# PSUM banks, the written order and the gate's rows between the output projection and the MLP of a hybrid layer

## The chip, the cores and the metric

The kernel runs on one core of a Trainium2 chip. The metric is device time in microseconds of one execution of the whole program; several executions are timed and the median is given. Beside them one execution is recorded by the hardware profiler, and all rows below are from that one. The engines are TensorE (PE, with its weight loads as PEld), VectorE (DVE), ScalarE (ACT), GpSimd (POOL) and SyncE (SP), which here only issues loads and stores.

## What is computed

One layer of a bidirectional trunk, 128 context and 512 latent tokens of width 1024. A token mixer of three head groups (differential attention, a gated linear recurrence, grouped-query attention) ends in one output projection, and an MLP with squared ReLU follows. What the change touches is from the projection on:

```python
def _layer(x, mod, lp, li, rope, ctx):
    sh1, sc1, g1, sh2, sc2, g2 = jnp.split(mod, 6, axis=-1)
    m, own = _token_mixer(x * (1.0 + sc1) + sh1, lp, li, rope, ctx)   # ends in mixed @ w_out
    x = _layernorm(ALPHA * x + g1 * m, lp['ln1_g'], lp['ln1_b'])
    hid = jnp.square(jax.nn.relu((x * (1.0 + sc2) + sh2) @ lp['w_ff1']))
    x = _layernorm(ALPHA * x + g2 * (hid @ lp['w_ff2']), lp['ln2_g'], lp['ln2_b'])
    return x, own
```

`w_ff1` is 1024 x 4096, `w_ff2` 4096 x 1024, all in float32.

## The kernel before, in words

A float32 operand is split into a high part (a cast, `A.copy` on ScalarE, L91, L1284, L1336) and a low part (a subtraction on VectorE, L92, L1287, L1340), and a product is three matmuls (high x high, high x low, low x high). The 640 tokens are five row tiles `t` of 128; tile 0 is the context.

**Projection (`wo_gemm`).** For each row tile and each half of the 1024 columns 24 matmuls sum into one PSUM bank (`pswo`). `residual` (L1226, L1230) reads that bank on VectorE, multiplies by the gate's row and adds to `xn`; `half_stats`, `norm_stats` and `normalize` (ScalarE, L1255 to L1258) follow in the second half. `turn(t)` transposes the normalised row tile on TensorE into two banks `psh{t}0` and `psh{t}1`, four blocks of 128 columns each, and `h2(t, q)` moves them into the quarters `raws[i, j]` (`q00` to `q11`) while it scales and shifts: `q=0` on ScalarE (L1281), `q=1` on VectorE (L1279).

**First MLP matrix.** It runs in 16 units `u` of 256 columns by Strassen's scheme in Winograd's form, seven products `m1` to `m7` of 12 matmuls each in place of eight. The activations' four sums `s1` to `s4` and quarters `a11`, `a12`, `a22` are made once (`sums12`, `sum_hi`, `sum_lo`); the weights' four sums `t1` to `t4` are made per unit by `b_sums` on VectorE (L1311 to L1313), and split by `hi_(u, what, ..)` and `lo_(u, what, ..)`. `keep(u, i)` copies a bank's state to SBUF on ScalarE (L1459); `c11`, `c12`, `c21`, `c22` add such copies to a bank and apply the squared ReLU (VectorE L1472 and L1467, or ScalarE L1464 and L1465); `store` parks the result in HBM. `m6(u)` adds to the bank that `keep(u,1)` has read, so it waits for that copy. Units 0 and 1 run interleaved in an order of their own, from unit 2 on a loop runs.

**Second MLP matrix.** Rows of the hidden layer come back from HBM (`hidb`), each is split (`gh`, `gl`, buffers of eight rows), each pair of weight blocks is loaded (`wg_..r`, two buffers) and split (`wg_..h`, `wg_..l`), and five banks `psy` sum over 32 rows, for one half `n` of the columns and then the other. The first four rows are taken from the end of the first matrix (`pair_gemm`). `gate_rows("g2", n)` spreads the second gate over the partitions by two matmuls (L1213) and two ScalarE copies (L1214); only the residuals after the last row need it.

**What sets the order.** From `region` on, TensorE, ScalarE, VectorE and SyncE run their instructions exactly as the code is written; outside it a list scheduler places them. `region.close()` stands before `gate_rows("g2", 0)`, so the scheduler placed that call. Each engine works off its queue in order, and an instruction that waits for another engine's count holds all that stand behind it. A PSUM tile's bank is given by the pools: `outps` has eight banks in turn, then `ffps` takes two banks for each of the tags `x`, `z`, `y`, `f`, in the order in which the tags are first asked for, and a tile may be written when all readers of the tile that had the bank before are done. In the program as built the last tiles lie so: row tile 3's projection (`pswo13`) in bank 7, `psh20` in 6, `psh21` in 7, `pswo14` in 4, `psy0` in 5, `psh30` and `psh31` in 6 and 7.

## Time and profile before

| | us |
|---|---|
| median of 3 runs (lowest, highest) | 940.05 (936.37, 941.13) |
| the profiled execution's own time | 940.01 |
| its span in the trace | 938.2 |
| PE / PEld / DVE / ACT / POOL busy | 880.3 / 762.6 / 665.1 / 474.9 / 69.0 |
| mean granted TensorE clock | 0.975 |

The span is the time from the first to the last instruction of the trace; 1.8 us of the execution lie outside it. A busy share is a mean over stages with different limits. The granted clock is given as a share of 2.4 GHz; 0.5 is 1.2 GHz.

### The profile page before, as it was taken

The numbers are of one execution on the slowest core, as the hardware profiler recorded it, in microseconds if no ns is written. First come the engines' busy times: TensorE is split into PE (matmuls) and PEld (weight loads), VectorE is DVE, ScalarE is ACT, GpSimd is POOL, SyncE is SP. The second block draws the span as 40 slices with busy tenths as digits, with TensorE's granted clock in tenths as the row PEclk, the third lists the DMA queues.
The fourth block names the chain that finished last, engine by engine and source line by source line (L and its number), as shares of the span: only waits on it lengthen the run. The fifth ranks groups of instructions, "written<-read, shape, count | busy, mean of one in ns | idle before, by whom it ended". The sixth has DMA issues, their size and how long they took to land.

```text
span 938.2 us, 15408 instructions
## 1 busy us (share of the span) xinstructions
PE 880.3 (94%) x5941; PEld 762.6 (81%) x5941; DVE 665.1 (71%) x1232; ACT 474.9 (51%) x973; POOL 69.0 (7%) x136
## 2 busy tenths in 40 slices
PE   5989898999999998999988899999998999999996
PEld 3878786789889786677778899988997888888885
DVE  2369997988876878886579877676762874574448
ACT  3567665466664638761566544453553633243320
POOL 2200010210101010001000100110000000000000
PEclk7999998999999999999999999999999999999998
DMA  9951525432122211007102543456325863052202
GB/s 261 287 168 50 179 71 146 118 95 69 55 58 62 68 51 57 2 28 274 36 1 64 186 145 134 157 176 208 129 79 188 295 218 99 22 177 90 67 22 92
DMA packets 102314, 109.84 MB, mean 117 GB/s; under 512 B 6720, under 2 KB 82208, under 8 KB 102240
## 3 DMA queue, kind: packets, MB, share of 16 engines
q1 hardware_dynamic: 96256, 92.33, 32.0%
q0 software_dynamic: 5792, 16.44, 5.0%
q8 instruction: 47, 0.77, 0.3%
q14 instruction: 27, 0.22, 0.1%
q10 hardware_dynamic: 192, 0.08, 0.0%
HBM read 96.24 MB, written 12.58 MB: 116 GB/s over the span
## 4 chain that ended last, share of the span: by engine, by line
PE 67%; DVE 15%; DMA 8%; ACT 6%; issue 3%; SPq 1%; DVEq 0%; ACTq 0%
PE psx L1453 10%; PE psy L131 8%; PE psy L129 8%; PE psy L130 8%; PE psz L1453 5%; DMA wad<-in_w_ada 3%; PE psA L130 2%; PE psA L129 2%; PE psA L131 2%; PE psavA L731 2%; DVE b_st L561 2%; PE psy L1453 2%; DMA wf_r<-in_w_ff 2%; PE psavC L953 1%; DVE b_lqk L516 1%
## 5 line engine op out<-in xcount | busy, mean ns | idle before, releaser
L92 DVE TENSOR_TENSOR gl<-hidb,gh 128x640 fp32r<-128x640 f32 x54 | 43.7, 821 | 49.1 <-ACT gh L91 49.0
L91 ACT CAST gh<-hidb 128x640 fp32r<-128x640 f32 x54 | 38.6, 728 | 69.3 <-PE psy L130 61.9
L1453 PE MATMUL psx<-s,wf3h 128*128 128x320 f32 x256 | 58.9, 317 | 6.2 <-ACT kept L1459 3.0
L129 PE MATMUL psA<-wa_h,xh 128*128 128x384 f32 x160 | 54.9, 344 | 0.0
L131 PE MATMUL psA<-wa_h,xl 128*128 128x384 f32 x160 | 54.5, 342 | 0.0
L130 PE MATMUL psA<-wa_l,xh 128*128 128x384 f32 x160 | 54.2, 340 | 0.0
L1459 ACT COPY kept<-psx 128x320 f32<-128x320 f32 x48 | 20.5, 427 | 65.6 <-PE psx L1453 65.6
L1453 PEld LDWEIGHTS psx<-s,wf3h 128*128 128x128 f32 x256 | 44.1, 193 | 7.0 <-ACT kept L1459 3.3
L1340 DVE TENSOR_TENSOR wf3l<-wf_t,wf3h 128x2048 fp32r<-128x2048 f32 (+2 forms) x20 | 37.2, 1864 | 9.0 <-ACT wf3h L1336 9.0
L1453 PE MATMUL psx<-s,wf3l 128*128 128x320 f32 x128 | 40.3, 315 | 0.0
L1472 DVE TENSOR_TENSOR st<-psz,kept 128x320 f32<-128x320 f32 x32 | 15.7, 489 | 26.2 <-ACT kept L1459 13.7
L129 PE MATMUL pswo<-wo,mxh 128*128 128x512 f32 x80 | 32.1, 403 | 0.4 <-ACT wo L91 0.4
L130 PE MATMUL pswo<-wo,mxh 128*128 128x512 f32 x80 | 31.7, 397 | 0.8 <-DVE wo L92 0.8
L709 DVE TENSOR_REDUCE nmA<-pssA 128x1 f32<-128x768 f32 x32 | 30.2, 951 | 2.2 <-PE pssA L707 1.8
L129 PEld LDWEIGHTS psA<-wa_h,xh 128*128 128x128 f32 x160 | 30.1, 188 | 1.9 <-issue 1.2
L1336 ACT CAST wf3h<-wf_t 128x2048 fp32r<-128x2048 f32 (+2 forms) x20 | 30.9, 1554 | 1.3 <-DVE wf_t L1312 0.9
L131 PE MATMUL pswo<-wo,mxl 128*128 128x512 f32 x80 | 31.5, 393 | 0.0
L1518 POOL DMA_DIRECT2D hd<-st x28 | 15.3, 546 | 219.3 <-ACT st L1465 120.4
L711 ACT ACTIVATE pA<-pssA,nmA 128x768 f32<-128x768 f32 x32 | 28.8, 903 | 3.3 <-DVE nmA L709 2.8
L130 PEld LDWEIGHTS psA<-wa_l,xh 128*128 128x128 f32 x160 | 30.2, 189 | 0.2
L131 PEld LDWEIGHTS psA<-wa_h,xl 128*128 128x128 f32 x160 | 30.1, 188 | 0.2
L1453 PE MATMUL psz<-s,wf3h 128*128 128x320 f32 x128 | 29.2, 315 | 0.0
(671 smaller groups left out, 2760.8 us busy)
## 6 DMA issues: line engine op xcount, KB each, us to landing
wad<-in_w_ada SPq DMA_DIRECT2D x32, 512.0 KB, 4.8
wf_r<-in_w_ff SPq DMA_DIRECT2D x32, 512.0 KB, 4.7
hd<-st POOLq DMA_DIRECT2D x28, 320.0 KB, 3.6
hidb<-hd SPq DMA_DIRECT2D x28, 320.0 KB, 4.7
adaw<-in_w_ada SPq DMA_DIRECT2D x32, 256.0 KB, 5.3
wa_r<-in_w_in SPq DMA_DIRECT2D x48, 128.0 KB, 2.7
wo_raw<-in_w_out SPq DMA_DIRECT2D x8, 512.0 KB, 6.5
x<-in_x_sample SPq DMA_DIRECT2D x8, 256.0 KB, 4.9
```

The source lines that it names most:

```text
L91: A.copy(hi, src)
L92: V.tensor_tensor(lo, src, f32(hi), op=ALU.subtract)
L129: PE.matmul(ps, s[0], m[0], start=start, stop=False)
L130: PE.matmul(ps, s[0], m[1], start=False, stop=False)
L131: PE.matmul(ps, s[1], m[0], start=False, stop=stop)
L561: V.scalar_tensor_tensor(dst, st[r, c, :], dec[r, c : c + 1], u(r, c), op0=ALU.mult, op1=ALU.add)
L709: V.tensor_reduce(nm, ps[:, 0:NKEY], axis=AX.X, op=ALU.max, negate=True)
L711: A.activation(pr, ps[:, 0:NKEY], AF.Exp, bias=nm, accum_out=sm[:, col : col + 1])
L1336: A.copy(h, src)
L1340: V.tensor_tensor(l, src, f32(h), op=ALU.subtract)
L1453: PE.matmul(ps, a_[:, k, :], b_[:, k, :], start=start and k == 0 and i == 0, stop=k == 3 and i == 2, skip_group_check=True)
L1459: A.copy(t, U[u].ps["x"][:, 0:HALF])
```

## The change

Five edits between the projection's second half and the end of unit 1, and one in the second matrix:

1. The tags of `ffps` are asked for in the order `x z f y` in place of `x z y f`. As built, `psh20` then lies in bank 4 and `psh21` in 5, `pswo14` in 6, `psy0` in 7, `psh31` in 5, `psh30` in 4. The banks' former tiles are those of row tile 1 and of the turn of tile 0; `pswo13` in bank 7 has `psy0` behind it.
2. `h2(0, 1)` runs on ScalarE and no longer on VectorE. `hi_(0, 3)` (the cast of unit 0's weight sums, 128 x 2048) stands before `h2(0, 0)` on ScalarE and no longer after `normalize(1)`. `lo_(0, 3)` keeps its place on VectorE.
3. The last turns: `turn` takes a list of quarters; tile 3's two are placed around `m2(0)`, tile 4's come before `m1(1)`. `h2(2, 1, 1)` comes before `residual(4)`, `h2(4, 1)` before the sums `s1` and `s2`; `keep(0, 1)` comes after tile 4's `h2` on ScalarE, and the cast `hi_(1, 3, 0, 2)` after `s1`'s.
4. The end of units 0 and 1: `b_sums` is cut into its first two and its last instruction. `c11(1)` moves from before `c22(1)` to after `c12(0)`, `b_sum4(2)` to after `lo_(2, 3, 0, 2)`, `c12(1)` to before `lo_(2, 3, 3, 4)`.
5. `gate_rows("g2", 0)` is called within the region, in the loop's pass for row 18.

```diff
-    def turn(t, bank="f"):
-        for q in range(2):
+    def turn(t, bank="f", qs=(0, 1)):
+        for q in qs:
...
-                if q:
+                if q and t:
                     V.tensor_scalar(dst, src, a2[:, kk, v : v + 1], b2[:, kk, v : v + 1], op0=ALU.mult, op1=ALU.add)
                 else:
                     A.activation(dst, src, AF.Identity, scale=a2[:, kk, v : v + 1], bias=b2[:, kk, v : v + 1])
...
     def b_sums(u, pool, tag):
+        b_sums3(u, pool, tag)
+        b_sum4(u)
+
+    def b_sums3(u, pool, tag):
         g = U[u]
         r = g.r
         g.t = t = pool.tile([P, 4, 4, P], F32, tag=tag, name=f"wf_t{u}")
         V.tensor_tensor(t[:, 0:2], r[:, :, :, 1, :], r[:, 0].rearrange("p k c n -> p c k n"), op=ALU.subtract)
         V.tensor_tensor(t[:, 2], r[:, 1, :, 1, :], t[:, 0], op=ALU.subtract)
-        V.tensor_tensor(t[:, 3], r[:, 1, :, 0, :], t[:, 2], op=ALU.subtract)
+
+    def b_sum4(u):
+        g = U[u]
+        V.tensor_tensor(g.t[:, 3], g.r[:, 1, :, 0, :], g.t[:, 2], op=ALU.subtract)
...
-            for b in "xzyf":
+            for b in "xzfy":
                 fps[0].tile([P, 512], F32, tag=b, name=f"ps_{b}")
...
             hi_(0, 2)
-            lo_(0, 3)
...
             normalize(0, mvs[0])
+            f3[0] = [wop.tile([P, 4, 4, P], F32R, tag=tag, name=f"wf3{p}0") for p, tag in (("h", "wr"), ("l", "w3"))]
+            hi_(0, 3)
         elif t == 1:
             h2(0, 0)
             h2(0, 1)
             normalize(1, mvs[1])
-            f3[0] = [wop.tile([P, 4, 4, P], F32R, tag=tag, name=f"wf3{p}0") for p, tag in (("h", "wr"), ("l", "w3"))]
-            hi_(0, 3)
+            lo_(0, 3)
...
             hi_(1, 2, 0, 1)
+            h2(2, 1, 1)
...
-    def c21(u):
+    def c21(u, last=True):
         relu2(st[:, u % 2, 0, HALF:NTOK], U[u].ps["x"][:, 0:HALF], True)
-        store(u, 0)
+        if last:
+            store(u, 0)
...
     m1(0)
-    keep(0, 1)
+    turn(3, qs=(1,))
+    m2(0)
     h2(2, 0, 1)
+    turn(3, qs=(0,))
     lo_(1, 1)
-    h2(2, 1, 1)
-    m2(0)
-    turn(3)
-    normalize(4, mvs[4])
-    m1(1)
-    turn(4, "z")
     h2(3, 1)
     lo_(1, 2, 0, 1)
+    normalize(4, mvs[4])
+    turn(4, "z")
+    h2(3, 0)
+    h2(4, 0)
+    h2(4, 1)
+    m1(1)
     m2(1)
-    h2(3, 0)
+    keep(0, 1)
     keep(1, 1)
     sums12(0, 192)
-    h2(4, 0)
-    h2(4, 1)
-    hi_(1, 3, 2, 3)
     parts("s2")
     sum_hi("s2", s2r, 0, 192)
-    hi_(1, 3, 0, 2)
+    hi_(1, 3, 2, 3)
...
     lo_(1, 3, 2, 3)
+    hi_(1, 3, 0, 2)
...
+    sum_hi("s4", s2r)
     c11(0)
-    sum_hi("s4", s2r)
...
     m3(0)
-    c11(1)
+    c21(1, False)
     c22(1)
-    c21(1)
     lo_(2, 1)
     m3(1)
+    b_sums3(2, wop, "w2")
+    hi_(2, 3, 2, 3)
+    lo_(2, 3, 2, 3)
     lo_(2, 2, 0, 1)
     c12(0)
-    b_sums(2, wop, "w2")
-    hi_(2, 3, 2, 3)
-    lo_(2, 3, 2, 3)
     hi_(2, 3, 0, 2)
+    c11(1)
+    store(1, 0)
     lo_(2, 3, 0, 2)
+    b_sum4(2)
     hi_(2, 3, 3, 4)
+    c12(1)
     lo_(2, 3, 3, 4)
     hi_(2, 2, 1, 2)
-    c12(1)
     lo_(2, 2, 1, 2)
...
+            if n == 0 and m == 20:
+                g2r = gate_rows("g2", 0, [fps[0].tile([P, 512], F32, tag=b, name=f"psabg2{b}") for b in "xy"])
             if n == 0 and m >= 8:
                 alpha_rows(m - 8)
...
             region.close()
-        g2r = gate_rows("g2", n, [fps[0].tile([P, 512], F32, tag=b, name=f"psabg2{b}") for b in "xy"] if n == 0 else None)
+        else:
+            g2r = gate_rows("g2", n)
```

TensorE before, from m1(0) to the start of m6(0). psx0 and psy0 are m1(0) and m2(0), psx1 and psy1 m1(1) and m2(1); psh3 and psh4 are the turns of row tiles 3 and 4.

```order
L1453 MATMUL psx0_5605<-a11_5333,b11_0_5123 128x320 x12
L1453 MATMUL psy0_5606<-a12_5334,wf12h_5471 128x320 x12
L1268 MATMUL psh30_5643<-ident_65,xn_5096 128x128 x4
L1268 MATMUL psh31_5648<-ident_65,xn_5096 128x128 x4
L1453 MATMUL psx1_5607<-a11_5333,wf12l_5472 128x320 x12
L1268 MATMUL psh40_5669<-ident_65,xn_5096 128x128 x4
L1268 MATMUL psh41_5674<-ident_65,xn_5096 128x128 x4
L1453 MATMUL psy1_5608<-a12_5334,wf12l_5472 128x320 x12
L1453 MATMUL psx0_5605<-s2_5712,wf3h0_5433 128x320 x2
```

The same place in the changed kernel.

```order
L1461 MATMUL psx0_5609<-a11_5333,b11_0_5123 128x320 x12
L1268 MATMUL psh31_5625<-ident_65,xn_5096 128x128 x4
L1461 MATMUL psy0_5610<-a12_5334,wf12h_5472 128x320 x12
L1268 MATMUL psh30_5646<-ident_65,xn_5096 128x128 x4
L1268 MATMUL psh40_5661<-ident_65,xn_5096 128x128 x4
L1268 MATMUL psh41_5666<-ident_65,xn_5096 128x128 x4
L1461 MATMUL psx1_5611<-a11_5333,wf12l_5473 128x320 x12
L1461 MATMUL psy1_5612<-a12_5334,wf12l_5473 128x320 x12
L1461 MATMUL psx0_5609<-s2_5711,wf3h0_5379 128x320 x2
```

All four turns now stand before unit 1's products, and none of the matmuls is new.

VectorE before, from s4's low part to the low part of unit 2's last weight quarter. The st rows with psz0, psy1 and psz1 are the sums of c22(0), c11(1), c22(1), c12(0) and c12(1) in that order; wf_t2 is b_sums(2).

```order
L1287 TENSOR_TENSOR s41_5821<-s2r_5603,s40_5820 128x1280
L1472 TENSOR_TENSOR st_5822<-psz0_5742,kept_5601 128x320
L1472 TENSOR_TENSOR st_5822<-psy1_5608,kept_5601 128x320
L1472 TENSOR_TENSOR st_5822<-psz1_5774,kept_5601 128x320
...
L1340 TENSOR_TENSOR wf12h_5471<-wf_r2_5723,wf12h_5471 128x512 x2
L1472 TENSOR_TENSOR st_5822<-psz0_5742,kept_5601 128x320
L1311 TENSOR_TENSOR wf_t2_5900<-wf_r2_5723 128x1024
L1312 TENSOR_TENSOR wf_t2_5900<-wf_r2_5723,wf_t2_5900 128x512
L1313 TENSOR_TENSOR wf_t2_5900<-wf_r2_5723,wf_t2_5900 128x512
L1340 TENSOR_TENSOR wf3l0_5434<-wf_t2_5900,wf3h0_5433 128x512
L1340 TENSOR_TENSOR wf3l0_5434<-wf_t2_5900,wf3h0_5433 128x1024
L1472 TENSOR_TENSOR st_5822<-psz1_5774,kept_5601 128x320
```

The same place in the changed kernel, from c22(1) on.

```order
L1480 TENSOR_TENSOR st_5822<-psz1_5774,kept_5605 128x320
L1347 TENSOR_TENSOR wf12h_5472<-wf_r2_5722,wf12h_5472 128x512
L1315 TENSOR_TENSOR wf_t2_5890<-wf_r2_5722 128x1024
L1316 TENSOR_TENSOR wf_t2_5890<-wf_r2_5722,wf_t2_5890 128x512
L1347 TENSOR_TENSOR wf3l0_5380<-wf_t2_5890,wf3h0_5379 128x512
L1480 TENSOR_TENSOR st_5822<-psz0_5742,kept_5605 128x320
L1480 TENSOR_TENSOR st_5822<-psy1_5612,kept_5605 128x320
...
L1347 TENSOR_TENSOR wf3l0_5380<-wf_t2_5890,wf3h0_5379 128x1024
L1320 TENSOR_TENSOR wf_t2_5890<-wf_r2_5722,wf_t2_5890 128x512
L1480 TENSOR_TENSOR st_5822<-psz1_5774,kept_5605 128x320
```

c11(1) went behind c12(0), the last weight sum behind the low part of the first two, and c12(1) ahead of the low part of the last.

ScalarE before, at the change to the second matrix. st is the last squared ReLU, g20 are the gate's rows, wg0_2h and gh0.. high parts of weights and hidden rows.

```order
L1464 ACTIVATE st_5822<-st_5822 128x320
L1465 ACTIVATE st_5822<-st_5822 128x320
L1214 COPY g200_8297<-psabg2x_8295 128x512
L1214 COPY g201_8300<-psabg2y_8296 128x512
L91 CAST wg0_2h_7740<-wg0_2r_7738 128x1024
L91 CAST gh02_7745<-hidb2_7712 128x640
```

ScalarE in the changed kernel, at the rows 17 to 20 of the second matrix.

```order
L91 CAST gh017_8107<-hidb17_7727 128x640
L91 CAST wg0_18h_8130<-wg0_18r_8128 128x1024
L91 CAST gh018_8135<-hidb18_7728 128x640
L1214 COPY g200_8141<-psabg2x_8139 128x512
L1214 COPY g201_8144<-psabg2y_8140 128x512
L91 CAST gh019_8165<-hidb19_7729 128x640
L91 CAST wg0_20h_8188<-wg0_20r_8186 128x1024
```

The two copies moved behind sixteen rows' casts; on TensorE their matmuls stand after row 17's, where before they stood before row 2's.

## Rows read from the trace of the kernel before

**Rows 1.** The page, part 1: busy time of each engine, its share of the span, and its instructions.

```profile
PE 880.3 (94%) x5941; PEld 762.6 (81%) x5941; DVE 665.1 (71%) x1232; ACT 474.9 (51%) x973; POOL 69.0 (7%) x136
```

**Rows 2.** Who waited for whom, TensorE alone, over the whole run: what waited, for what, us in total, times, longest us. Of the rows left out between the first and the second, one is m6(0)'s (3.0 us, on s L1284); one of them and one ahead of the third belong to the first half of the program.

```profile
PE psx L1453 <- ACT kept L1459: 3.0, 1, 3.0
...
PE psh L1268 <- DVE 1.18920711500272131_5542 L1226: 2.6, 1, 2.6
...
PE psy L129 <- ACT gh L91: 2.5, 1, 2.5
```

**Rows 3.** TensorE in order of time, 474 to 546 us: start us, us, engine, line, operation, out<-in, count, and in brackets the idle time before it and what ended it. The psh rows are the turn of row tile 2; pswo at 479 to 485 is the projection of row tile 4; psx<-a,b is m1(0); psx<-s,wf3h at 498 and 499 are the first two matmuls of m6(0), at 524 the first of m6(2).

```profile
475.34 0.66 PE L1268 MATMUL psh<-ident,xn 128*128 128x128 f32 x4 [0.24 <-ACT xn L1258]
478.64 1.11 PE L1268 MATMUL psh<-ident,xn 128*128 128x128 f32 x4 [2.64 <-DVE 1.18920711500272131_5542 L1226]
479.40 0.77 PE L129 MATMUL pswo<-wo,mxh 128*128 128x512 f32 x1
...
482.01 0.40 PE L130 MATMUL pswo<-wo,mxh 128*128 128x512 f32 x1
...
485.65 0.39 PE L131 MATMUL pswo<-wo,mxl 128*128 128x512 f32 x1
485.88 1.92 PE L1453 MATMUL psx<-a,b 128*128 128x320 f32 x12
...
498.41 0.63 PE L1453 MATMUL psx<-s,wf3h 128*128 128x320 f32 x1 [2.97 <-ACT s L1284]
499.23 0.63 PE L1453 MATMUL psx<-s,wf3h 128*128 128x320 f32 x1 [0.19 <-DVE s L1287]
...
524.66 0.56 PE L1453 MATMUL psx<-s,wf3h 128*128 128x320 f32 x2 [3.02 <-ACT kept L1459]
```

**Rows 4.** Stretches of 2 us, 460 to 534 us: stretch and its length, then busy time (and instructions) of PE, PEld, DVE, ACT, POOL, then the granted TensorE clock, DMA share and GB/s.

```profile
478.00:480.00 2.00, 1.36 (x6) 1.27 (x7) 1.93 (x3) 0.00 (x0) 0.00 (x0) 0.50 0.00 0
480.00:482.00 2.00, 2.00 (x7) 1.59 (x6) 1.74 (x8) 1.59 (x4) 0.00 (x0) 0.66 0.00 0
...
524.00:526.00 2.00, 1.34 (x8) 1.34 (x9) 1.93 (x3) 2.00 (x4) 0.54 (x1) 0.94 0.41 95
526.00:528.00 2.00, 2.00 (x10) 2.00 (x9) 2.00 (x3) 1.57 (x2) 0.00 (x0) 0.50 1.01 315
```

**Rows 5.** All engines in order of time, 462 to 500 us, columns as in rows 3; of it ScalarE and VectorE around the first turned tile. L1281 and L1279 are h2 on ScalarE and on VectorE, L1336 and L1340 hi_ and lo_, L1258 the end of normalize, L1226 the first step of a residual.

```profile
462.85 1.51 ACT L1281 ACTIVATE q<-psh,b,a 128x128 f32<-128x128 f32 x4 [0.75 <-PE psh L1268]
...
465.46 1.25 ACT L1258 ACTIVATE xn<-xn,mva 128x1024 f32<-128x1024 f32 x1
466.61 1.89 ACT L1336 CAST wf3h<-wf_t 128x2048 fp32r<-128x2048 f32 x1
468.53 2.29 DVE L1340 TENSOR_TENSOR wf3l<-wf_t,wf3h 128x2048 fp32r<-128x2048 f32 x1 [2.53 <-ACT wf3h L1336]
470.74 0.68 DVE L1226 TENSOR_TENSOR 1.18920711500272121_5475<-pswo,g 128x512 f32<-128x512 f32 x1
```

**Rows 6.** VectorE in order of time, 474 to 546 us, columns as in rows 3: the residuals of row tiles 3 and 4, the low part (two pieces) that m6(0) waits for, and s4's low part.

```profile
477.90 0.68 DVE L1226 TENSOR_TENSOR 1.18920711500272131_5542<-pswo,g 128x512 f32<-128x512 f32 x1
...
486.08 0.69 DVE L1226 TENSOR_TENSOR 1.18920711500272141_5592<-pswo,g 128x512 f32<-128x512 f32 x1 [2.88 <-PE pswo L131]
...
497.62 1.55 DVE L1287 TENSOR_TENSOR s<-s2r,s 128x768 fp32r<-128x768 f32 x2
...
511.69 1.49 DVE L1287 TENSOR_TENSOR s<-s2r,s 128x1280 fp32r<-128x1280 f32 x1 [0.41 <-ACT s L1284]
```

**Rows 7.** ScalarE in order of time, 474 to 546 us, columns as in rows 3: normalize(4)'s end, the first square of c12(1), and the copy keep(2,1) that m6(2) waits for.

```profile
490.24 1.24 ACT L1258 ACTIVATE xn<-xn,mva 128x1024 f32<-128x1024 f32 x1
...
523.32 0.47 ACT L1464 ACTIVATE st<-st 128x320 f32<-128x320 f32 x1 [1.26 <-DVE st L1472]
...
524.20 0.41 ACT L1459 COPY kept<-psx 128x320 f32<-128x320 f32 x1
```

**Rows 8.** TensorE in order of time, 698 to 732 us, columns as in rows 3: the gate's first matmul, and the first and the thirteenth matmul of the next pair of hidden rows.

```profile
719.13 0.39 PE L1213 MATMUL psabg2x<-grows,sel 128*128 128x512 f32 x1
...
722.25 0.50 PE L129 MATMUL psy<-wg_2h,gh 128*128 128x512 f32 x1 [2.50 <-ACT gh L91]
...
727.13 0.40 PE L130 MATMUL psy<-wg_2l,gh 128*128 128x512 f32 x1
```

**Rows 9.** ScalarE in order of time, 698 to 745 us, columns as in rows 3: the first of the gate's copies and the first cast of that pair.

```profile
719.56 0.59 ACT L1214 COPY g<-psabg2x 128x512 f32<-128x512 f32 x1 [9.64 <-PE psabg2x L1213]
...
720.52 1.06 ACT L91 CAST wg_2h<-wg_2r 128x1024 fp32r<-128x1024 f32 x1
```

**Rows 10.** SyncE's queue in order of time, 698 to 745 us: the issue of the first loads of that pair (start us, us of the issue).

```profile
708.41 0.38 SPq L1760 DMA_DIRECT2D wg_2r<-in_w_ff  x1
708.84 0.94 SPq L1764 DMA_DIRECT2D hidb<-hd  x2
```

**Rows 11.** All work on the tiles hidb between 705 and 730 us, its last row: time of a load from issue to landing.

```profile
DMA to landing us min/median/max: 4.3/5.2/8.8
```

**Rows 12.** All work on the tile wg_2r, its last row: time of that load from issue to landing.

```profile
DMA to landing us min/median/max: 3.6/3.7/3.7
```

**Rows 13.** Groups of instructions between 730 and 800 us: line, engine, operation, out<-in, count | busy us, mean ns of one | idle time of the engine just before, and what ended it.

```profile
L92 DVE TENSOR_TENSOR gl<-hidb,gh 128x640 fp32r<-128x640 f32 x21 | 17.2, 822 | 14.9 <-ACT gh L91 14.8
L91 ACT CAST gh<-hidb 128x640 fp32r<-128x640 f32 x20 | 14.5, 727 | 29.2 <-PE psy L130 25.3 <-DVE wg_16l L92 2.7 <-DMA hidb<-hd 1.2
```

## The prediction

> **What bounds the kernel now.** I read the busy shares first, then the waits of TensorE, then its instructions in order of time at the three waits that the edits touch. TensorE is busy for 880.3 of 938.2 us [rows 1], so a gain must come from its idle time or from stretches at the lower clock. Two of the three waits shown lie before m6(2) and before the second pair of hidden rows, the third is that of a turn [rows 2]. In order of time the reader sees how each begins: `psh21` may only be written when `residual(3)` has read bank 7, which it begins at 477.90 [rows 6], so TensorE idles 2.64 us and then runs the projection's last row tile at first at a clock of 0.50 and 0.66 [rows 3, 4]; before m6(2) it idles 3.02 us for `keep(2,1)` [rows 3]; and before the second pair it idles 2.50 us [rows 8], because ScalarE stood 9.64 us in front of the gate's copies [rows 9].
>
> **The turn's wait.** After the change `psh21` lies in a bank whose tile has long been read, and `pswo14` starts when the turn ends. `psh20` started at 475.34 [rows 3]; two turns of 0.4 us and a slip of 0.3 (below) put that at 476.1 against 479.40. A matmul at the full clock takes 0.2275 us, (485.65 - 482.01) / 16 [rows 3]; 24 take 5.46 us, where the slow start made them 6.48, 479.40 to 485.88 [rows 3]. m1(0) then starts at 481.6 in place of 485.88: **-4.3 us**.
>
> **What moves ahead of it.** ScalarE is free at 462.10, since it idled 0.75 us before 462.85 [rows 5]. It now does the cast (1.89) first, then two `h2` of 1.51 each [rows 5] where VectorE did the second. `normalize(1)` fills the time from the end of `h2(0,0)`, 464.36, less waits 2.14 us, to 466.71 [rows 5]; behind cast and both `h2` it ends near 468.85. Turn 1 is late by the 0.3 us used above. In return VectorE no longer waits 2.53 us before `lo_(0,3)`, and `residual(2)` starts near 468.8, not 470.74 [rows 5]. So VectorE reaches `residual(3)` earlier too, at some 476.5 against 477.90 [rows 6], and nothing that TensorE needs before m1(0) comes later.
>
> **How much reaches m6(0).** `residual(4)` waits for the projection (2.88 us of idle) and starts at 486.08 [rows 6]. It now stands behind `h2(2,1,1)`, 1.1 us, and starts near 482.8. `normalize(4)` ended at 491.48 [rows 7], held up by an `h2` and a copy that stood ahead of it on ScalarE; it ends near 487.3, TensorE turns tile 4 there, `h2(4,1)` follows at 488.5 to 489.9, the four sums end at 493.1, and the low part that m6(0) waits for at 494.5 in place of 499.17 [rows 6]. The second matmul of m6(0) goes from 499.23 [rows 3] to 494.6, -4.6 us. TensorE waits some 0.7 us longer in total there than before, since the turn of tile 4 now is waited for. The VectorE chain keeps this: `s4`'s low part ended at 513.18 [rows 6]; I take 508.3, **-4.9** (-4.6 to -5.3).
>
> **The end of units 0 and 1 gives some back.** From there to `keep(2,1)` it took 11.0 us, 513.18 to 524.20 [rows 6, 7]. In the new order VectorE waits twice for a ScalarE cast, which itself stands behind the relu of c12(0) and the squares of c12(1) (0.47 us each [rows 7]); I get 0.75 and 1.1 us of such idle, less 0.5 us of work moved behind the copy: 12.4 us. `keep(2,1)` then starts at 520.7 and m6(2) at 521.1 instead of 524.66 [rows 3]: **-3.6 us** net. TensorE reaches this point early and waits 4.5 to 4.9 us in place of 3.02, so its idle time hardly shrinks; VectorE's and ScalarE's chain is the bound here, and what edit 1 saves on TensorE is worth only what it saves on that chain. If the new order costs nothing the term is -4.9; if the shorter TensorE time only turns into waiting, it is 0. I choose -3.6 as the value that follows from walking the queues. From unit 2 on TensorE is the bound, and the shift is kept.
>
> On the restart rows show a clock of 0.94 in the first 2 us after the 3.02 us wait and 0.50 in the next two [rows 4]. So the wait already costs the low clock, some 1.8 us, and a longer wait costs it once more, not twice; I price it at zero difference. The Trainium skill, page "TensorE: Matmul & The Clock Gate", section "What's actually happening", says that the throttled state is the default and that activity releases it; by that rule a longer wait restarts every one of m6(2)'s matmuls at the low clock, and the term would be -2.5 by my estimate in place of -3.6. The 0.94 shows that this trace did not do so after 3.02 us.
>
> **The gate's rows.** Before, ScalarE stands from 709.9 to 719.56 in front of the copies, because their matmuls wait in TensorE's queue to 719.13 [rows 8, 9]. The loads for the next pair were issued at 708.41 and 708.84 [rows 10] and land 3.7 us [rows 12] and 4.3 to 8.8 us later [rows 11], at the latest at 717.6. So without the copies the casts are done before TensorE comes, and it goes on at 719.12 at the full clock. The thirteenth matmul of the pair, where it is back at the full rate, comes at 719.12 + 12 x 0.2275 = 721.85 rather than 727.13 [rows 8]: -5.28, less 0.46 for the two gate matmuls, which still run later: **-4.8 us**. Bounds: -3.0 (the wait alone is gone, the slow clock stays) and -5.3.
>
> **What it costs at row 18.** The copies now stand in ScalarE's queue behind row 18's cast and wait for TensorE to end row 17 (T). All later casts wait with them, and the lead of up to eight rows shrinks to one. The first row's cast follows 1.07 us (719.56 to 720.52 and the rest of the second copy [rows 9]) after T, then 0.73 and 0.82 us for high and low part [rows 13]; with semaphores row 19 is complete at T + 3.0, needed at T + 15 x 0.2275 + 0.46 = T + 3.87. The hard place is the end of the half: its last eight rows are summed bank by bank, so the first bank wants the last weight pair (rows 30 and 31) at T + 18.7. ScalarE has five pairs to do by then, each 1.06 + 2 x 0.73 = 2.52 us [rows 9, 13], 14.4 us with the copies, so 4 us are spare. But the pairs' loads have two buffers, and two loads in series lie before rows 30 and 31; with 3.7 us a load [rows 12] I walk the queues to T + 18.8. I take **+0.4** (0 to 1). If each of these loads takes 8.8 us [rows 11], it is 2 x 5.1 = 10.2 more, a wait of some 9 us and 2 more for the clock. The Trainium skill, page "PSUM — Partial Sum Buffer", section "Engine vs sequencer instructions", speaks against this edit: ScalarE's queue is strict first in, first out, so no ready cast may pass the waiting copy. The 9.64 us in front of one copy agree [rows 9]; by the rule the price above is due anew, at a place with more lead.
>
> The rest (stores, the order of c11 and c12, banks of later tiles) I cost at nothing: VectorE and ScalarE have idle time there behind a busy TensorE, and were that cover gone it would be the 0.5 us per moved instruction.
>
> **Sum.** 938.2 - 3.6 - 4.8 + 0.4 = 930.2 us of span; 1.8 us lie outside it: **932.0 us**. The profiled execution (940.01) stands at the median (940.05), so nothing is shifted.
>
> **Rivals.**
> - *The first stretch gains nothing:* the chain on VectorE and ScalarE keeps its time (the waits for the casts grow by all that is won), 935.6. For it: TensorE waits for other engines at both m6(0) and m6(2) [rows 3]. Against: `residual(4)` itself waits 2.88 us for TensorE [rows 6].
> - *More gain:* the end of units 0 and 1 costs nothing and row 18 neither, 930.3; without the restart's 1.8 us 928.5. Against it: the added waits follow from the queues.
> - *The lead is worth more than I think:* row 18 gives back 2.5 to 6 us, 934.2 to 938. For it: weights have two buffers, and my margin is 0.1 us.
> - *Slower:* the loads behind T take 8.8 us as the slowest did [rows 11], the last pair is 9 us late, and TensorE restarts slowly: +11 in place of +0.4, 942.6; with the first stretch at nothing as well 946. It decides, against the two gains of 8.4, once wait and clock exceed 8.4 us. Against it: the loads of weights took 3.7 us.
>
> **Chances.** Forecast (930 to 934.2) 0.58; no gain in the first stretch 0.13; more gain 0.09; lead worth more 0.14; slower 0.06. Leaving out a part of the slower and of the extreme cases gives 928.5 to 937.5. The bound between a change and none is 0.5%, what a measurement of this kernel can tell: 935.35 and 944.75. Faster: 0.58, 0.09, half of the first rival and a third of the lead's, 0.78; slower by more than that only the sum of two mishaps, 0.04; 0.18 within.
>
> **What would show it.** Right: no wait at `psh`'s second turn and a clock of 1.0 in the projection's last row tile; m1(0) near 481.6; m6(0) near 494; m6(2) near 521 behind a wait of over 4 us; no wait of ScalarE at 709, the second pair starting at the full clock right behind the first; ScalarE idle before `g` at row 18, and TensorE's wait near the last weight pair below 1 us. Wrong: m6(2) at 524 again, or a wait of several us for `gh` or `wg` in the last eight rows of the first half.

## The result, and the profile after

The changed kernel takes 933.02 us (median of 8 executions, 932.00 to 935.48), the kernel before 940.99 us in the same comparison: a ratio of 0.9917 (95% interval 0.9894 to 0.9941). The prediction was 932.0, range 928.5 to 937.5. The execution that was profiled took 932.00 us, the shortest of the eight, with a span of 930.2 us; predicted was a span of 930.2.

The page's first part, which answers to [rows 1]:

```profile
PE 878.0 (94%) x5941; PEld 760.8 (82%) x5941; DVE 663.0 (71%) x1228; ACT 475.9 (51%) x977; POOL 69.0 (7%) x136
```

TensorE's busy share did not move; what went is waiting and low clock. TensorE's waits over the whole run, cut to those behind the projection (columns as in [rows 2]):

```profile
PE psx L1461 <- ACT kept L1467: 4.5, 1, 4.5
...
PE psx L1461 <- ACT s L1284: 1.8, 1, 1.8
...
PE psh L1268 <- ACT xn L1258: 1.0, 1, 1.0
```

The waits for the residual and for `gh` in [rows 2] are gone, and the wait for `keep(2,1)` grew from 3.0 to 4.5 us. TensorE in order of time shows where (columns as in [rows 3], which answer to these rows; the last three are in the place of [rows 8]):

```profile
474.88 1.03 PE L1268 MATMUL psh<-ident,xn 128*128 128x128 f32 x8
475.67 0.48 PE L129 MATMUL pswo<-wo,mxh 128*128 128x512 f32 x1
...
481.24 1.92 PE L1461 MATMUL psx<-a,b 128*128 128x320 f32 x12
...
486.81 1.09 PE L1268 MATMUL psh<-ident,xn 128*128 128x128 f32 x8 [1.02 <-ACT xn L1258]
...
494.03 0.41 PE L1461 MATMUL psx<-s,wf3h 128*128 128x320 f32 x1 [0.41 <-DVE s L1287]
...
521.25 0.56 PE L1461 MATMUL psx<-s,wf3h 128*128 128x320 f32 x2 [4.45 <-ACT kept L1467]
...
715.60 0.39 PE L131 MATMUL psy<-wg_p,g 128*128 128x512 f32 x1
715.82 0.39 PE L129 MATMUL psy<-wg_2h,gh 128*128 128x512 f32 x1
...
718.09 0.39 PE L130 MATMUL psy<-wg_2l,gh 128*128 128x512 f32 x1
```

Both halves of turn 2 run in one piece, m1(0) starts at 481.24 (485.88 in [rows 3]), m6(0)'s second matmul at 494.03 (499.23), m6(2) at 521.25 (524.66), and the second pair of hidden rows follows the first without a gap. On VectorE and ScalarE, rows that answer to [rows 6, 7] and to the gate's copy in [rows 9]:

```profile
482.22 0.68 DVE L1226 TENSOR_TENSOR 1.18920711500272141_5596<-pswo,g 128x512 f32<-128x512 f32 x1
...
506.84 1.49 DVE L1287 TENSOR_TENSOR s<-s2r,s 128x1280 fp32r<-128x1280 f32 x1 [0.40 <-ACT s L1284]
...
513.34 0.69 DVE L1347 TENSOR_TENSOR wf3l<-wf_t,wf3h 128x512 fp32r<-128x512 f32 x1 [0.69 <-ACT wf3h L1343]
...
517.02 1.23 DVE L1347 TENSOR_TENSOR wf3l<-wf_t,wf3h 128x1024 fp32r<-128x1024 f32 x1 [1.05 <-ACT wf3h L1343]
```

```profile
520.78 0.42 ACT L1467 COPY kept<-psx 128x320 f32<-128x320 f32 x1
...
770.66 0.58 ACT L1214 COPY g<-psabg2x 128x512 f32<-128x512 f32 x1 [23.54 <-PE psabg2x L1213]
```

The first turn, that of row tile 0, starts at 462.16 us in the trace of before and at 461.86 in this one; over all traces of this study its start lies between 460.1 and 465.1. What makes it differ was not traced. So stages are compared from that start on, which removes this spread. The table gives, in us, the start of m1(0), of m6(0)'s second matmul and of m6(2) after the first turn, then from m6(2) to the thirteenth matmul of the second pair, from there to TensorE's last matmul, and the whole from the first turn to the span's end (the span is read to 0.1 us). "Low clock" is the time lost at a granted clock under 1.00 around m6(0) and around m6(2): over stretches of 1 us, TensorE's busy time times (1 - clock), summed.

| kernel | m1(0) | m6(0) | m6(2) | to pair 2 | to last | turn to end | low clock |
|---|---|---|---|---|---|---|---|
| before | 23.72 | 37.07 | 62.50 | 202.94 | 201.59 | 476.04 | 1.5, 1.7 |
| changed | 19.38 | 32.17 | 59.39 | 197.29 | 202.63 | 468.34 | 1.7, 1.7 |
| changed, again | 19.40 | 32.17 | 58.27 | 197.85 | 203.14 | 468.34 | 0, 3.0 |
| gate_alone | 22.46 | 35.81 | 61.60 | 196.92 | 202.96 | 470.54 | 1.7, 1.7 |
| no_gate | 19.41 | 32.17 | 59.39 | 202.17 | 201.56 | 472.19 | 1.7, 1.7 |
| end_old | 19.41 | 32.15 | 57.95 | 197.59 | 203.10 | 467.70 | 1.7, 2.9 |
| banks_alone | 19.54 | 34.08 | 60.86 | 204.23 | 201.57 | 475.72 | 3.1, 3.1 |
| edit2_off | 19.57 | 33.76 | 59.86 | 196.90 | 203.49 | 469.29 | 0, 1.4 |
| gate_m23 | 19.38 | 32.15 | 59.38 | 196.24 | 202.86 | 467.57 | 1.7, 1.7 |
| keep2_early | 19.41 | 32.16 | 54.78 | 201.81 | 202.83 | 468.45 | 1.7, 1.7 |
| keep4_early | 19.39 | 32.16 | 54.77 | 198.20 | 202.48 | 464.54 | 1.7, 0 |
| keep5_early | 19.40 | 32.19 | 54.81 | 198.46 | 203.63 | 465.91 | 1.7, 0 |

Of the 8.0 us by which the span shrank, 0.30 lie ahead of the first turn, far inside the spread there, and are not counted as the change's. The rest is -3.11 to m6(2), -5.65 to the second pair, +1.04 behind it: -7.7.

### The profile page after: what moved, and what is told of

Its sections match the earlier page's. It is cut to its first block, busy times and chain, and to the rows that moved or that the text cites. A ratio compares the mean times of both kernels' runs of the same rounds, so it can differ in the third digit from the quotient of the medians.

```text
span 930.2 us, 15406 instructions
## 1 busy us (share of the span) xinstructions
PE 878.0 (94%) x5941; PEld 760.8 (82%) x5941; DVE 663.0 (71%) x1228; ACT 475.9 (51%) x977; POOL 69.0 (7%) x136
## 4 chain that ended last, share of the span: by engine, by line
PE 70%; DVE 11%; DMA 8%; ACT 6%; issue 2%; SPq 1%; DVEq 0%; ACTq 0%
PE psx L1461 10%; PE psy L129 8%; PE psy L131 8%; PE psy L130 8%; PE psz L1461 5%; DMA wad<-in_w_ada 4%; PE psA L130 2%; PE psA L129 2%; PE psA L131 2%; PE psavA L731 2%; PE psy L1461 2%; DMA wf_r<-in_w_ff 2%; PE psavC L953 1%; DVE b_st L561 1%; PE pstA L721 1%
```

## The experiments

**Which edit gives what.** `gate_alone` is the kernel before with edit 5, `no_gate` the changed kernel without it.

```diff
+            if n == 0 and m == 20:
+                g2r = gate_rows("g2", 0, [fps[0].tile([P, 512], F32, tag=b, name=f"psabg2{b}") for b in "xy"])
...
-        g2r = gate_rows("g2", n, [fps[0].tile([P, 512], F32, tag=b, name=f"psabg2{b}") for b in "xy"] if n == 0 else None)
+        else:
+            g2r = gate_rows("g2", n)
```

> The kernel before with edit 5 alone. The two gains are independent (theory): the second pair's thirteenth matmul moves from 727.13 to about 722, span 938.2 - 4.8 = 933.4, nothing lost at row 18, and the stretch 474 to 526 as before (m6(2) near 524.7). Rival (the lead is worth more): TensorE waits 2 to 6 us for gh or wg in the last eight rows of the first half, span 935 to 939.

Measured: 936.21 us (12 executions) against 940.19, ratio 0.9952 (0.9930 to 0.9973). From m6(2) to the last matmul 399.88 us (196.92 + 202.96) against 404.53 before, -4.65; TensorE waits once more in the last eight rows, 0.31 us for `gh`. The gain is edit 5's own and comes as expected.

This run also tells something of the trace of before. Up to the second matrix the two kernels run the same instructions, and the waits ahead of m6(2) are the same (2.65, 2.97 and 3.03 us here, 2.64, 2.97 and 3.02 there). Yet m1(0) comes 1.26 us earlier here and m6(2) 0.90, because the clock stayed at 1.00 behind the wait at turn 2, where it fell in the trace of before (the rows are at the end). So 0.9 of the 3.11 us that edits 1 to 4 gain up to m6(2) hang on how the clock happened to go in that one trace; against this run they gain 2.21.

> The changed kernel without edit 5 (edits 1 to 4 alone). Theory: m6(2) near 521.25 as in the changed kernel, the 2.5 us wait before the second pair and its slow start are back, span 938.2 - 3.6 = 934.6. Rival (the first stretch's gain is lost again behind unit 2): span 937 or more.

Measured: 937.35 us (12 executions), ratio 0.9981 (0.9960 to 1.0001); the span is 935.8, and from the first turn to the end it is 3.85 us shorter than before, 3.11 of them ahead of m6(2). The wait of 2.50 us for `gh` is back. So in the trace the first stretch's gain is kept to the end. The times alone show it less well, since their interval just reaches 1. The two gains add up: 0.48% and 0.19% against 0.83% together, within their intervals.

**The end of units 0 and 1 (`end_old`).** The changed kernel with edit 4's lines replaced by those of before:

```diff
-    c21(1, False)
     c22(1)
+    c21(1)
     lo_(2, 1)
     m3(1)
-    b_sums3(2, wop, "w2")
-    hi_(2, 3, 2, 3)
-    lo_(2, 3, 2, 3)
     lo_(2, 2, 0, 1)
     c12(0)
...
```

> The changed kernel with edit 4 undone (the end of units 0 and 1 in the order of before). Theory (the new order there costs 1.4 us): keep(2,1) near 519.3, 11.0 us behind s4's low part, m6(2) near 519.8 in place of 521.25, span 930.2 - 1.4 = 928.8. Rival (the new order is what carries the gain through): m6(2) at 521.3 or later, span 930.2 to 932.

Measured: m6(2) at 57.95 after the first turn, 1.44 earlier than in the changed kernel; expected was 1.4. But the time hardly follows: 467.70 from the first turn to the end (-0.64), median 932.34 us (6 executions), ratio to before 0.9911 (0.9883 to 0.9939). Behind its wait of 3.02 us the low clock lasted longer:

```profile
520.00:522.00 2.00, 0.25 (x1) 0.26 (x2) 2.00 (x3) 1.56 (x4) 0.33 (x1) 0.71 0.00 0
522.00:524.00 2.00, 2.00 (x8) 2.00 (x9) 1.93 (x4) 1.56 (x3) 0.21 (x1) 0.50 0.84 235
524.00:526.00 2.00, 2.00 (x9) 2.00 (x9) 1.97 (x4) 1.82 (x2) 0.00 (x0) 0.50 1.05 369
526.00:528.00 2.00, 2.00 (x10) 2.00 (x9) 2.00 (x2) 0.00 (x0) 0.00 (x0) 0.59 0.80 226
```

The column behind POOL is the granted clock (columns as in [rows 4]). In the changed kernel m6(2) starts at 521.25 at the full clock and loses it later and for less time:

```profile
520.00:522.00 2.00, 0.75 (x5) 0.75 (x6) 1.31 (x3) 2.00 (x5) 0.54 (x1) 1.00 0.14 54
522.00:524.00 2.00, 2.00 (x10) 2.00 (x9) 1.93 (x3) 0.67 (x1) 0.00 (x0) 0.51 0.84 243
524.00:526.00 2.00, 2.00 (x11) 2.00 (x11) 2.00 (x4) 1.78 (x1) 0.00 (x0) 0.63 1.05 363
```

The low clock took 1.2 us more than in the changed kernel (2.9 against 1.7). That is not quite the whole account: to the second pair only 0.30 us are lost, since TensorE is idle 0.6 us less on the way, and behind it another 0.47, nearly all a wait of 0.43 us for `gh` at the last weight pair. No run shows that edit 4 gains anything: at m6(2) it costs 1.4 us, and the median without it is 0.7 us lower, which is within the spread.

**The banks alone (`banks_alone`).**

```diff
-            for b in "xzyf":
+            for b in "xzfy":
```

> The kernel before with edit 1 alone (the order in which the PSUM tags are asked for). Theory (VectorE's and ScalarE's chain bounds the stretch, and the bank frees it only as far as residual(4) comes earlier): no wait at the second half of turn 2, m1(0) near 481.6 (-4.3), residual(4) near 483.2 behind the sums of a12 (-2.9), m6(0) and m6(2) 2.5 to 3 us earlier, span 935.2 to 935.7. Rival 1 (TensorE's time counts as it is): all of -4.3, span 933.9. Rival 2 (the bank alone only moves the wait): m6(2) within 1 us of 524.66, span 937.5 or more.

Measured: m1(0) 4.18 us earlier, m6(0) 2.99, m6(2) only 1.64, from the first turn to the end 0.32; median 938.93 us (12 executions), ratio 0.9985 (0.9965 to 1.0004), which the times can't tell from none. TensorE's 4.2 us turn into 3.0 at m6(0), as theory had it from `residual(4)`'s place on VectorE. The rest of the way the low clock took it back in this trace: 3.1 us lost at either restart in place of 1.5 and 1.7, 1.6 and 1.4 us more, which is about what is missing. That part was in neither theory. Of the 4.18 us at m1(0), 1.26 are the low clock behind the wait, as `gate_alone` shows; against that run the banks alone give 2.92 at m1(0) and 1.73 at m6(0).

**Edit 2 (`edit2_off`).**

```diff
-                if q and t:
+                if q:
...
-            f3[0] = [wop.tile([P, 4, 4, P], F32R, tag=tag, name=f"wf3{p}0") for p, tag in (("h", "wr"), ("l", "w3"))]
-            hi_(0, 3)
         elif t == 1:
             h2(0, 0)
             h2(0, 1)
             normalize(1, mvs[1])
-            lo_(0, 3)
+            f3[0] = [wop.tile([P, 4, 4, P], F32R, tag=tag, name=f"wf3{p}0") for p, tag in (("h", "wr"), ("l", "w3"))]
+            hi_(0, 3)
```

> The changed kernel with edit 2 undone (h2(0,1) back on VectorE, hi_(0,3) and lo_(0,3) where they stood before). Theory (edit 2 frees VectorE, which sets when residual(4) runs): VectorE waits 2.5 us for the cast again, residual(4) comes 1.5 to 2 us later behind h2(2,1,1), and m6(0) and m6(2) with it, counted from the first turn; m1(0) stays within 0.4 us. Span 1.5 to 2 us above the changed kernel's, counted from the first turn. Rival (it only delays turn 1): all of it 0.3 us earlier.

Measured: m1(0) 0.19 us and m6(0) 1.59 us later, as the theory says, m6(2) 0.47 and the end 0.95 later: this time no low clock followed the 1.77 us wait before m6(0) (0 against 1.7 us), which hid most of the loss. Median 933.86 us (10 executions), ratio 0.9937 (0.9918 to 0.9956). With `banks_alone`: of the 4.9 us at m6(0), the banks give 3.0 (1.3 of it the clock at turn 2) and edit 2 about 1.6; 0.3 are left for edit 3, which was not run alone.

**What the lead at row 18 is worth (`gate_m23`).**

```diff
-            if n == 0 and m == 20:
+            if n == 0 and m == 23:
```

> The changed kernel with the gate's rows three rows later (in the pass of row 21). Theory (each row later takes from the lead that the last eight rows need): TensorE waits 4 to 6 us for the last weight pairs and then runs at the low clock for 1.7 to 3 us: 6 to 9 us slower than the changed kernel behind m6(2). Rival (the casts catch up, the lead costs nothing): within 0.7 us.

Measured: 931.87 us (6 executions), ratio 0.9916 (0.9895 to 0.9938), from the first turn to the end 0.77 us *less* than the changed kernel; behind the second pair 202.86 against 202.63. The theory's 6 to 9 us did not come. TensorE's order shows what it had not reckoned with. The last eight rows are issued behind the region, where the list scheduler places them, and it wove the second and third bank's products in between the first's where the casts come late. TensorE in that kernel, behind row 21 (matmuls, bank, hidden row):

```
2 psy00 row 22, 1 psy01 row 22, 1 psy00 row 22, 3 psy00 row 23, 1 psy00 row 24, 2 psy01 row 22,
1 psy01 row 23, 1 psy00 row 24, 2 psy01 row 23, 1 psy00 row 24, 3 psy00 row 25, 3 psy01 row 24, ...
```

Before, bank 0's 24 products stand in one piece; in the changed kernel three of bank 1's stand between them. The casts did come late, as the theory has it. On ScalarE the cast of the last weight pair (rows 30 and 31), in the changed kernel and in this one:

```profile
786.81 1.05 ACT L91 CAST wg_30h<-wg_30r 128x1024 fp32r<-128x1024 f32 x1 [0.93 <-DMA wg_30r<-in_w_ff]
...
790.90 1.05 ACT L91 CAST wg_30h<-wg_30r 128x1024 fp32r<-128x1024 f32 x1 [1.06 <-DMA wg_30r<-in_w_ff]
```

Counted from the thirteenth matmul of the second pair (718.54 and 717.85) it ends at 69.3 and at 74.1 us, 4.8 later, and the pair's first product starts at 70.0 and at 75.0. TensorE has no wait over 0.15 us in between: it worked on the other banks. That the other order is what absorbs the delay follows from this, but a run with the order of these rows held fixed was not made.

**Where the wait before m6(2) comes from.** The prediction called the chain on VectorE and ScalarE the bound of that stretch. Five kernels move ScalarE's copies for TensorE ahead of casts that wait for VectorE, one wait after the other. `keep21_early`:

```diff
     c12(0)
+    banks(2)
+    m1(2)
+    keep(2, 1)
     hi_(2, 3, 0, 2)
```

> The changed kernel with the copy keep(2,1) ahead of the cast hi_(2,3,0,2) in ScalarE's queue, nothing else moved. Theory (VectorE's and ScalarE's chain is the bound): m6(2) starts without a wait, near 55 us after the first turn in place of 59.4, but m7(2) then waits some 5 us for keep(2,2), which stands behind a cast of unit 3 that waits for VectorE; from m1(3) on the time is within 1 us of the changed kernel's. Rival (that copy's place in the queue is the bound): the 4.5 us wait and 1.7 us of low clock are gone, 6 us faster.

Measured: no wait at m6(2), which comes near 55 us, but 6.47 us at m7(2), and a loss of 3.1 us at the low clock behind it; 3.05 us slower from the first turn to the end (471.39), median 935.38 us (7 executions), 0.9954 (0.9933 to 0.9975). The wait moved as theory said and cost 2 us more than it said.

```profile
526.96 0.90 PE L1461 MATMUL psx<-s,wf3h 128*128 128x320 f32 x2 [6.47 <-ACT kept L1467]
```

`keep2_early` adds

```diff
+    m2(2)
+    m6(2)
     b_sum4(2)
     hi_(2, 3, 3, 4)
+    keep(2, 2)
     c12(1)
...
+            hi_(3, 1)
+            lo_(3, 1)
+            b_sums(3, wop, "w2")
```

> As keep21_early, and keep(2,2) ahead of the squares of c12(1), with the low part of unit 3's first quarter ahead of its sums on VectorE. Theory: no wait before m6(2) and m7(2); the VectorE chain then sets m3(2), since c22(2) stands behind lo_(3,3); 1.5 to 4 us faster than the changed kernel from the first turn to the end, not more. Rival 1 (queue places alone were the bound): 6 us faster. Rival 2 (the chain has no slack at all): within 0.7 us.

Measured: 468.45 from the first turn to the end, as the changed kernel; median 934.44 us (6 executions), 0.9935 (0.9912 to 0.9959). By its number rival 2 holds, but not by its reason: the next copy waited, m4(2)'s `keep(2,3)`, behind a cast that waits for unit 3's sums, and the clock fell behind it (1.7 us).

```profile
529.54 0.56 PE L1461 MATMUL psx<-a,wf3h 128*128 128x320 f32 x2 [3.11 <-ACT kept L1467]
```

`keep3_early` puts `m5(2)`, `m7(2)`, `keep(2, 3)` ahead of `b_sums(3)` and `c22(2)` right behind it.

> As keep2_early, and m5(2), m7(2) and keep(2,3) ahead of unit 3's sums, c22(2) ahead of lo_(3,2) and lo_(3,3). Theory (each copy that TensorE waits for stands behind a cast that waits for VectorE; VectorE itself has some 3 us of idle time per unit to catch up in): the 3.1 us wait before m4(2) goes, and the next wait is the one before m7(3), whose copy stands behind hi_(4,3), some 3 us; 1 to 3 us faster than the changed kernel from the first turn to the end. Rival (VectorE's amount of work is the bound): within 0.7 us of it.

Measured: the wait is now m7(3)'s, 3.3 us, as expected, and 3.4 us were lost at the low clock behind it; 470.44 from the first turn to the end, 2.1 us slower than the changed kernel where 1 to 3 faster was expected. Median 932.80 us (9 executions), 0.9930 (0.9905 to 0.9954): on the same chip the changed kernel has 932.62, so over several executions this kernel is neither slower nor faster, and the trace's 2.1 us are within what the low clock alone makes of a restart.

`keep4_early` puts the cast of the next unit's sums behind the copy in every later unit:

```diff
             lo_(u + 1, 2)
-            hi_(u + 1, 3)
+            if u == 2:
+                hi_(u + 1, 3)
...
             m6(u)
             keep(u, 2)
+            if more:
+                hi_(u + 1, 3)
```

> As keep3_early, and from unit 3 on the cast hi_(u+1,3) stands behind keep(u,2) on ScalarE. Theory (queue places, one after the other, are the bound): no wait of TensorE over 0.7 us from m6(2) to the end of unit 15, the second restart at the low clock gone; 4.5 to 6 us faster than the changed kernel from the first turn to the end, span near 924 to 926. Rival (VectorE's amount of work is the bound): TensorE waits for low parts (wf3l or wf12) in units 3 to 5, and the gain is under 2 us.

Measured: no low clock behind m6(2) any more, 3.80 us faster than the changed kernel from the first turn to the end (4.5 to 6 expected); median 929.53 us (6 executions, 929.02 to 931.76), ratio to before 0.9896 (0.9868 to 0.9924), where the changed kernel on the same chip gave 932.62 and 0.9927. The expectation that no wait over 0.7 us is left did not come true; two waits of TensorE in units 2 and 3 matter:

```profile
PE psx L1461 <- ACT kept L1467: 1.5, 1, 1.5
...
PE psx L1461 <- DVE wf3l L1347: 0.5, 1, 0.5
```

Queue places, not VectorE's amount of work, were the larger part of the bound: 3.8 of the 6.2 us that the changed kernel lost there (4.45 of waiting, 1.7 of low clock).

`keep5_early` moves `c11(2)` behind `lo_(3, 3)` and unit 4's sums behind the sum of `c12(2)` on VectorE.

> As keep4_early, and on VectorE c11(2) behind lo_(3,3), and the sum of c12(2) ahead of unit 4's sums. Theory: the waits left in keep4_early, 0.48 us before m6(3) (for a low part) and 1.55 us before m7(3) (for a copy behind the squares of c12(2)), go; from the first turn to the end 462 to 463 us against 464.5 there and 468.3 in the changed kernel. Rival (the wait moves on to unit 4): within 0.7 us of keep4_early.

Measured: both waits gone; median 926.73 us (6 executions), ratio 0.9834 (0.9807 to 0.9861): faster than both kernels. The profiled one of them was the slowest (932.43; the other five 922.52 to 927.36). In the middle units TensorE waits for the loads of the gate's weights there; the changed kernel has these waits too (0.88 and 0.79 us), but here the clock fell behind them:

```profile
615.62 0.64 PE L144 MATMUL psadag<-wad,cs 128*32 128x256 f32 x8 [1.08 <-DMA wad<-in_w_ada]
617.06 0.92 PE L144 MATMUL psadag<-wad,cs 128*32 128x256 f32 x8 [0.80 <-DMA wad<-in_w_ada]
```

```profile
617.00:618.00 1.00, 0.94 (x9) 0.25 (x9) 0.00 (x0) 0.00 (x0) 0.00 (x0) 0.64 0.00 0
618.00:619.00 1.00, 1.00 (x4) 1.00 (x5) 0.50 (x2) 0.41 (x1) 0.26 (x1) 0.50 0.00 0
619.00:620.00 1.00, 1.00 (x6) 1.00 (x5) 0.97 (x3) 0.00 (x0) 0.80 (x2) 0.50 0.73 162
620.00:621.00 1.00, 1.00 (x6) 1.00 (x6) 1.00 (x2) 0.00 (x0) 0.00 (x0) 0.65 1.09 385
```

That is 0.94 x 0.36 + 0.50 + 0.50 + 0.35 = 1.69 us at the low clock. It and 1.15 us more behind the second pair (203.63 against 202.48 in `keep4_early`, 0.53 of it a wait for `gh`) are why this one trace stands at 465.91 from the first turn to the end where 462 to 463 was expected; without them it is 463.1.

**The changed kernel again (`after_again`).** The two kernels named in its expectation are `keep3_early` and `keep4_early`.

> The changed kernel once more, on the chip of the two above, to set them against it. From the first turn to the end 468.3 us as in its first trace, if the granted clock falls at the same places; 1.3 us more where a stretch at the low clock is the longer kind (3.0 us of loss in place of 1.7).

Measured: 932.62 us (9 executions), and 468.34 from the first turn to the end as before. The same instructions had another clock. After the wait of 1.77 us before m6(0) (1.78 in the first trace) the clock stayed:

```profile
494.00:496.00 2.00, 2.00 (x15) 1.90 (x14) 2.00 (x3) 2.00 (x4) 0.00 (x0) 1.00 0.00 0
496.00:498.00 2.00, 2.00 (x16) 2.00 (x15) 2.00 (x3) 0.75 (x2) 0.00 (x0) 1.00 0.57 172
```

where the changed kernel's first trace, at the same matmuls, has

```profile
494.00:496.00 2.00, 1.97 (x9) 1.97 (x10) 1.65 (x2) 2.00 (x4) 0.00 (x0) 0.69 0.00 0
496.00:498.00 2.00, 2.00 (x9) 2.00 (x9) 2.00 (x3) 0.85 (x3) 0.00 (x0) 0.50 0.38 100
```

Behind m6(2) it is the other way round: 3.0 us lost here, 1.7 there. That both traces come to 468.34 us is chance.

## Why the prediction was right

**The turn's wait: right.** No wait at the turn's second half; `pswo14` at 475.67 (476.1 predicted), m1(0) at 481.24 (481.6). From the first turn it is 4.34 us earlier, predicted 4.3. `banks_alone` shows that the bank order alone does it (4.18). The term holds 1.0 us for the low clock behind the wait (6.48 against 5.46). That is a fact of the trace of before and not of the kernel: in `gate_alone` the same wait cost no clock.

**How much reaches m6(0): right.** `residual(4)` at 482.22 (482.8), TensorE's wait before turn 4 1.02 us (1.4), m6(0)'s second matmul at 494.03 (494.6), `s4`'s low part done at 508.33, 506.84 + 1.49 (508.3). From the first turn on that is 4.55 earlier, where the term was 4.9: the 0.3 us between the two traces' first turns account for nearly all of the difference. So the forecast times, counted from the span's start, fit better than the gain does.

**The end of units 0 and 1: right in its size.** From `s4`'s low part to `keep(2,1)` it took 12.45 us (520.78 - 508.33); 12.4 was predicted, with two idle times of VectorE of 0.75 and 1.1 us; the rows show 0.69 and 1.05. `end_old` confirms the price from the other side. The net term was -3.6 and measured -3.11. What was too simple is the sentence that VectorE's and ScalarE's chain is the bound: in this order it is, but `keep4_early` issues the same instructions with other places in the queues and is 3.8 us faster.

**The gate's rows: right, with a miscount.** The matmul at 727.13 in [rows 8] is the eleventh of its pair, not the thirteenth. Done right, the term is 719.12 + 10 x 0.2275 - 727.13 = -5.73, and -5.27 with the gate's two matmuls, in place of -4.8. Measured from m6(2) to that matmul: 718.09 - 521.25 = 196.84 against 727.13 - 524.66 = 202.47, -5.63, and with 0.46 for the gate -5.17.

**Row 18: right, but the margin is not the edge that it was taken for.** +0.4 was predicted; behind the second pair it is 1.04 longer, 0.46 of that the gate's matmuls and 0.58 slower matmuls at the last weight pair (0.26 to 0.36 us from one to the next in place of 0.23). The walk of the queues held. ScalarE stood 23.54 us in front of the copy with all casts behind it, and from the gate's first matmul (T) to the end of the last pair's low part it took 787.89 + 1.23 - 770.23 = 18.9 us, 18.8 predicted:

```profile
770.23 0.39 PE L1213 MATMUL psabg2x<-grows,sel 128*128 128x512 f32 x1
...
787.89 1.23 DVE L92 TENSOR_TENSOR wg_30l<-wg_30r,wg_30h 128x1024 fp32r<-128x1024 f32 x1 [0.74 <-ACT wg_30h L91]
```

TensorE came to that pair at T + 18.3 rather than T + 18.7 (788.54). What does not hold is the step from there to a wait: the prediction takes the first bank's 24 products to stay in one piece, so that every us beyond the margin is waited for, and `gate_m23`, with the casts 4.8 us later, shows that it is not.

**The restart's clock: right in two traces, not as a rule.** "Costs the low clock once more, not twice" held in the two profiled executions (1.7 and 1.7 us), and over all runs the loss after a single wait of 1.5 to 6.5 us was 0, 1.4 to 1.7, or 2.9 to 3.4. By the rule of the Trainium skill, page "TensorE: Matmul & The Clock Gate", section "What's actually happening" (throttled by default, released by activity), m6(2) would have restarted wholly at the low clock; the changed kernel's first trace does not agree (1.00 in its first stretch behind the 4.45 us), `end_old`'s does (0.71 and 0.50 from the start). Which one comes was not settled here.

**The hit on the total: in part luck.** The terms came out at -3.11, -5.2 and +0.58 us where -3.6, -4.8 and +0.4 were predicted; the sum is 0.3 short, and the 0.30 us ahead of the first turn, which no edit explains, close the gap. The miscounted matmul made the second term too small by about what the first was too large. And 0.9 us of the first hang on the clock at turn 2 in the one trace of before.

**The rivals.** No gain in the first stretch: refuted by the traces of `no_gate` and `gate_alone`, where m6(2) comes 59.39 and 61.60 us after the first turn; the medians point the same way without being clear of noise. A lead worth more, and the slower one by late loads: refuted by `gate_m23` as far as the place of the copies goes. More gain: part of it was to be had, not from this change but from the queue places.

## What to carry to other kernels

When a tile waits for its bank, look which tile had the bank before and who reads it last; asking for pool tags in another order costs no instruction and gave 2.9 us at the next product, 4.2 where the clock had fallen behind the wait, but each stage behind passed on less of it. An in-order queue turns one late operand into a wait for every ready operation behind it: copies that the bound engine waits for belong ahead of casts that wait for a third engine, and such waits have to be removed in a row, since one alone moves to the next copy (medians 935.4, 934.4, 932.8, 929.5 and 926.7 us in five steps, from 932.6 to 933.0). Compare stages from a common event late in the program when its beginning varies by more than the effect, and take a second trace before a difference of 1 to 3 us behind a wait is put down to an edit.

## What the runs showed of the hardware

The granted clock after the same wait of the same instructions differs from execution to execution. Behind a wait of 1.77 or 1.78 us before m6(0) it stayed at 2.4 GHz in one execution of the changed kernel and fell to 1.2 GHz in another (0 and 1.7 us lost); behind waits of 3.02 and 3.03 us before m6(2) 1.7, 1.7, 2.9 and 3.1 us were lost (before, `gate_alone`, `end_old`, `banks_alone`), behind 4.45 and 4.76 us 1.7 and 3.0 (the changed kernel twice). So each restart carries up to some 3 us that belong to no edit, as much as edits 1 to 4 bring together: the trace of `banks_alone` lost nearly all its gain to it, and that of `edit2_off` hid most of its loss. In `gate_alone` the clock also stayed at 1.00 behind a wait of 2.65 us at turn 2, where before it fell to 0.50 behind 2.64 [rows 3, 4]:

```profile
480.00:482.00 2.00, 1.56 (x9) 1.38 (x10) 1.90 (x4) 0.00 (x0) 0.00 (x0) 1.00 0.00 0
482.00:484.00 2.00, 2.00 (x11) 1.63 (x10) 1.58 (x7) 1.78 (x4) 0.00 (x0) 1.00 0.00 0
```

What decides it stays open; no run here held the waits and varied only their place.
